# A planner's assumptions about transfer time and instruction time, in a hybrid DeltaNet and attention layer on one core

## The chip, the cores and the metric

The kernel runs on one core of a Trainium2 chip. The metric is device time in microseconds (us); below, the median of several executions. Five engines take part, each with a queue that it works through strictly in order: PE (TensorE, matmul), DVE (VectorE), ACT (ScalarE), POOL (GpSimd) and SP (SyncE), which here issues all the transfers.

## The reference

One layer over a sequence of 2048 rows of width 1024, in float32. After an RMS norm one projection feeds two groups of heads, whose outputs are concatenated, projected and added to the input:

```python
h = rms_norm(x, norm_w)
proj = h @ w_in
(dn_q, dn_k, dn_v, dn_z, dn_beta, dn_decay, sw_q, sw_k, sw_v, sw_z) = split(proj)
# A: 4 heads of 128, gated delta rule, forward and backward over the sequence
qkv = silu(depthwise_conv5(concat(dn_q, dn_k, dn_v)))
t_inv = inverse(eye + tril(k_beta @ k.T * decay, -1))      # per chunk
v_new = u_i - w_i @ state                                  # scan over chunks
state = state * exp(g_last) + k_dec.T @ v_new
dn = rms_norm(fwd + bwd, dn_out_norm_w) * silu(dn_z)
# B: 8 query heads of 64 over 2 kv heads, window |i-j| <= 128, rotary, sink logit
sw = windowed_gqa_with_sinks(sw_q, sw_k, sw_v, ...) * silu(sw_z)
out = x + concat(dn, sw) @ w_out
```

## The kernel before

The sequence is cut into 16 chunks of 128 rows. Products that need precision are split: an operand is rounded by ACT to a high part in the type fp32r, DVE takes the rest as a low part, and PE does three matmuls (high by high, low by high, high by low) in place of one.

**Phase A** (to about 680 us) loads and normalises x (`xprep_rows`, `xprep`), projects keys and values (`pq_kv`, L210 to L212), queries (`pq_q`) and the feature-major columns (`pf_c`, `pf_z`, L199 to L201), applies the convolution as four DVE instructions per 512 columns (`acc`, L269), and does the window attention chunk by chunk (`attend`). Projected keys and values go to DRAM and come back in `kv_chunk` (`kv<-kv_d`, L327, then an ACT copy into `v2`, L330).

**Phase B** is a chain over the four DeltaNet heads. For head h, `pre_front(h)` transposes keys and values and forms the matrices (`gh` on PE, L702, then `ma` on DVE, L711; four of them sit in tiles called `xhi_h` and `xlo_h`), and stores them to DRAM (`m_d`, L716). `solve(h)` loads 32 by 32 blocks (`X`, `L`, L739 and L740) and inverts them on DVE in 31 steps of two instructions (`tm`, L749; `X`, L753). The result goes through DRAM (`x_d<-X`, L754; `xc<-x_d`, L765) into `invert(h)`, where DVE transposes (`xt`, L766) and copies blocks (`iv`, L776) and PE joins them (`pi`, L781). `scan(h)` then walks 16 steps in both directions (`pk`, `py`, `po` on PE; `r`, L823, and the state `S`, L842, on DVE; each step's `kqc` is loaded by L819). Names carry the head, direction and step: `r0_0_11` is head 0, forward, step 11. Meanwhile 32 units of the output projection of the attention half stand ready to fill PE (`unit`: load `mxs`, ACT `mhs`, DVE `mls` L591, load `xrs`, 12 matmuls `pcs` L596 to L598, DVE add into `xrs` L599, store `part`). Gate projections of phase A (`late_gates`: `zs`, `zhi`, `zlo`, `pf_z`, `zo`) fill PE around the first solve. At the end `out_pair` multiplies the DeltaNet half.

The order in which each engine sees its instructions is not the order of this text. `set_order` collects all instructions with their dependencies, gives each a duration (`cost`), gives each edge between engines a lag (`LAG`, `SAME`), and list-schedules them, several times backward and forward (`plan`). The best of the later forward plans becomes a chain of order-only dependencies on every engine (`add_manual_dep`). For a transfer the lag from issue to landing is `LAG["SP"]` plus `move`, the time on the planner's bus, both in ns:

```python
move[k] = count / piece * (8 + 0.148 * piece) / 16
lag = LAG[eng[k]] + move[k] + late[k] if k < n else 0
```

`count` is the transfer's elements and `piece` the contiguous run, at most 2048. No order is recorded across engines: on the chip an instruction starts when its own queue reaches it and its operands are there. So the planner's numbers cost no device time themselves; they only decide what stands behind what.

## Time and profile before

| | |
|---|---|
| median of 3 runs | 1264.82 us (1262.38 to 1266.28) |
| profiled execution, span | 1268.0 us |
| PE busy | 1210.5 us (95%) |
| DVE busy | 953.7 us (75%) |
| ACT busy | 725.8 us (57%) |
| POOL busy | 529.2 us (42%) |
| transfers | 206.39 MB, 163 GB/s over the span |
| mean granted PE clock | 0.989 |

The profiled execution's own time is its span; the median of the runs is 3.2 us below it. A busy share is a mean over stages: in phase A PE and, in the convolution, DVE are busy nearly all the time, in phase B PE waits at single places. Matmuls overlap in the record, so a PE that reads as busy need not be at its peak; start-to-start distances tell its pace. An idle time of an engine stands in brackets in a timeline, with what ended it.

### The profile page before, as it was taken

To read this page: it belongs to the slowest core of one execution; us is meant where nothing else is said; L and a number is where in the kernel's file an instruction comes from. 1 tells how busy PE (TensorE), PEld (TensorE's weight loads), DVE (VectorE), ACT (ScalarE), POOL (GpSimd) and SP (SyncE) were. 2 spreads that over 40 slices of the span, in tenths; PEclk is the share of its full clock that TensorE was granted. 3 is DMA by queue.
4 is the path that set the end of the run, shared out by engine and by line. 5 is a ranking of instruction groups with operands and counts; after the bars stand their busy time and mean duration, and the time that the engine had idled before them with its cause. 6 is when DMAs were issued, how large, how long until landed. Compare 5 with 4: busy or idle time off the path is not lost.

```text
span 1268.0 us, 22351 instructions
## 1 busy us (share of the span) xinstructions
PE 1210.5 (95%) x7018; PEld 1037.4 (82%) x7018; DVE 953.7 (75%) x2320; ACT 725.8 (57%) x2167; POOL 529.2 (42%) x845
## 2 busy tenths in 40 slices
PE   6999999999999999999999998999889899999898
PEld 5998888788889988887777777888789689888776
DVE  4523689999854379999995587698769779876765
ACT  6432476666534367766665438658557845685421
POOL 2243454763302276556422304613742441670541
PEclk9999999999999999999999999999889999999999
DMA  7553243513544434431016848967955875854785
GB/s 259 172 160 125 75 154 100 173 60 102 166 145 125 144 110 137 137 96 55 34 51 207 238 141 245 264 189 207 268 166 174 236 200 152 242 175 122 238 269 199
DMA packets 232294, 206.39 MB, mean 163 GB/s; under 512 B 49137, under 2 KB 181873, under 8 KB 232177
## 3 DMA queue, kind: packets, MB, share of 16 engines
q1 hardware_dynamic: 232176, 204.97, 53.0%
q8 instruction: 56, 0.92, 0.3%
q14 instruction: 62, 0.50, 0.1%
HBM read 139.84 MB, written 65.08 MB: 162 GB/s over the span
## 4 chain that ended last, share of the span: by engine, by line
PE 67%; DVE 13%; DMA 9%; ACT 4%; issue 3%; POOL 1%; SPq 1%; DVEq 0%; ACTq 0%; POOLq 0%
PE pf_c L199 5%; PE pf_c L201 5%; PE pf_c L200 5%; PE pf_z L199 4%; PE pf_z L200 4%; PE pf_z L201 4%; PE pi L781 3%; PE pq_q L212 2%; PE pq_q L211 2%; PE pt L390 2%; PE pq_q L210 2%; DMA xc<-x_d 2%; PE py L830 2%; PE po L839 2%; PE pcs L596 2%
## 5 line engine op out<-in xcount | busy, mean ns | idle before, releaser
L199 PE MATMUL pf_c<-xhi,wh_c 128*128 128x512 f32 x384 | 155.7, 405 | 0.8 <-DVE acc L269 0.8
L200 PE MATMUL pf_c<-xlo,wh_c 128*128 128x512 f32 x384 | 154.7, 403 | 0.0
L201 PE MATMUL pf_c<-xhi,wl_c 128*128 128x512 f32 x384 | 154.3, 402 | 0.0
L269 DVE SCALAR_TENSOR_TENSOR acc<-pf_c,cw,acc 128x512 f32<-128x512 f32 (+1 forms) x192 | 140.8, 742 | 2.6 <-POOL acc L259 0.7
L385 POOL TENSOR_SCALAR pr<-pr,st 128x384 f32<-128x384 f32 (+1 forms) x128 | 79.4, 639 | 98.0 <-DVE st L383 71.2
L394 ACT ACTIVATE ph<-pt 128x512 fp32r<-128x512 f32 x92 | 53.0, 595 | 60.5 <-PE pt L390 51.5
L376 ACT ACTIVATE pr<-pr,st 128x384 f32<-128x384 f32 (+1 forms) x128 | 76.2, 597 | 17.8 <-DVE st L372 17.4
L199 PEld LDWEIGHTS pf_c<-xhi,wh_c 128*128 128x128 f32 x384 | 72.5, 189 | 13.5 <-DVE acc L269 1.3
L201 PEld LDWEIGHTS pf_c<-xhi,wl_c 128*128 128x128 f32 x384 | 72.3, 188 | 12.9
L200 PEld LDWEIGHTS pf_c<-xlo,wh_c 128*128 128x128 f32 x384 | 72.4, 188 | 11.6
L835 ACT ACTIVATE yk<-py,ck 128x128 f32<-128x128 f32 x120 | 43.9, 366 | 62.0 <-PE py L830 61.2
L372 DVE CUSTOM_DVE_ANT_0 pr<-s,mask,sink 128x384 f32<-128x384 f32 (+1 forms) x128 | 73.4, 593 | 2.5 <-PE s L371 1.0
L211 PE MATMUL pq_q<-wh_q,xlo 128*128 128x256 f32 x256 | 72.1, 282 | 0.0
L212 PE MATMUL pq_q<-wl_q,xhi 128*128 128x256 f32 x256 | 71.9, 281 | 0.0
L210 PE MATMUL pq_q<-wh_q,xhi 128*128 128x256 f32 x256 | 71.4, 280 | 0.0
L390 PE MATMUL pt<-ident,pr 128*128 128x128 f32 x368 | 69.5, 274 | 1.8 <-DVE pl L395 1.1
L395 DVE TENSOR_TENSOR pl<-pt,ph 128x512 fp32r<-128x512 f32 x92 | 61.6, 681 | 6.1 <-ACT ph L394 5.6
L390 PEld LDWEIGHTS pt<-ident,pr 128*128 128x128 f32 x368 | 47.8, 140 | 20.4 <-DVE pl L395 4.4
L596 PE MATMUL pcs<-wohs,mhs 128*128 128x512 f32 x128 | 58.3, 456 | 4.4 <-ACT mhs L590 2.7
L692 POOL TENSOR_TENSOR nk<-ssk,pw 128x4 f32<-128x4 f32 x16 | 16.5, 1029 | 106.8 <-DVE ssk L691 106.6
L597 PE MATMUL pcs<-wohs,mls 128*128 128x512 f32 x128 | 56.1, 438 | 1.7 <-DVE mls L591 1.7
L598 PE MATMUL pcs<-wols,mhs 128*128 128x512 f32 x128 | 55.0, 429 | 0.0
(324 smaller groups left out, 4029.4 us busy)
## 6 DMA issues: line engine op xcount, KB each, us to landing
kqc<-kq_d SPq DMA_DIRECT2D x120, 128.0 KB, 3.1
ws_c<-wt SPq DMA_DIRECT2D x48, 256.0 KB, 3.5
xr<-x SPq DMA_DIRECT2D x16, 512.0 KB, 5.3
k_q<-kq_d SPq DMA_DIRECT2D x16, 512.0 KB, 5.6
mxs<-mix_sw SPq DMA_DIRECT2D x32, 256.0 KB, 3.7
xrs<-x SPq DMA_DIRECT2D x32, 256.0 KB, 3.7
part<-xrs SPq DMA_DIRECT2D x32, 256.0 KB, 2.6
xrd<-part SPq DMA_DIRECT2D x32, 256.0 KB, 4.1
```

Of the source, the lines that this page charges most:

```text
L199: T.matmul(ps, hi[:, k, cs], xhi[b][:, k], start=(k == 0), stop=False)
L200: T.matmul(ps, hi[:, k, cs], xlo[b][:, k], start=False, stop=False)
L201: T.matmul(ps, lo[:, k, cs], xhi[b][:, k], start=False, stop=(k == KC - 1))
L210: T.matmul(ps[:, :n], xh, hi[:, k, :n], start=(k == 0), stop=False)
L211: T.matmul(ps[:, :n], xl, hi[:, k, :n], start=False, stop=False)
L212: T.matmul(ps[:, :n], xh, lo[:, k, :n], start=False, stop=(k == KC - 1))
L269: V.scalar_tensor_tensor(av, ps[:, lo:], cw[:, i, k : k + 1], av, ALU.mult, ALU.add)
L372: V.tensor_tensor_reduce(pr[j][:, :n], ps[:, :n], mask[:, lo * P : hi * P], 1.0, sink[:, hh : hh + 1], ALU.add, ALU.min, accum_out=nm[:, j ...
L376: A.activation(pr[j][:, :n], pr[j][:, :n], AF.Exp, bias=nm[:, j : j + 1], scale=-1.0, accum_out=den[:, j : j + 1])
L385: G.tensor_scalar(pr[j][:, :n], pr[j][:, :n], den[:, j : j + 1], 1.0, ALU.mult, ALU.mult)
L390: T.transpose(pt[:, j], pr[j][:, (kb - lo) * P : (kb - lo + 1) * P], ident)
L596: T.matmul(ps, mh[:, k], wh[:, k], start=(k == 0), stop=False)
```

## The change

The planner gets other numbers; no instruction is added, taken out or altered. The lag of a transfer goes from 2400 to 3000 ns and its bus time is multiplied by 1.1. The cost of an ACT instruction gets a base by its source (45 ns from PSUM, 85 from SBUF, where it was 60), and other additions for a scalar operand, for a second output and for a strided PSUM source. POOL gets a cheaper broadcast multiply (1.6 in place of 2.1 ns per element), a cheaper copy on up to 32 partitions, and a cost for small two-tensor instructions that grows up to 8 elements instead of 4. A matmul in fp32r goes from 0.441 to 0.445 ns per column.

```diff
-LAG = {"PE": 205, "DVE": 140, "Activation": 160, "Pool": 120, "SP": 2400}
+LAG = {"PE": 205, "DVE": 140, "Activation": 160, "Pool": 120, "SP": 3000}
...
-                return max(112, 0.441 * m + 4)
+                return max(112, 0.445 * m + 4)
...
-            short = len(o[0].ap) > 2 and o[0].ap[-1][1] <= 64
-            return 60 + 0.86 * m + 85 * (scalars > 0) + 110 * (len(o) > 1) + 100 * short
+            src = ins[0]
+            psum = src.tensor.name in tiles and "PSUM" in str(tiles[src.tensor.name].space)
+            apart = psum and len(src.ap) > 2 and src.ap[-2][0] > src.ap[-1][1]
+            return (45 if psum else 85) + 0.86 * m + 100 * (scalars > 0) + 85 * (len(o) > 1) + 110 * apart
...
-            return 350 + 165 * min(m, 4) if m <= 16 else 180 + 2.1 * m
-        return 190 + 1.02 * m
+            if m <= 16:
+                return 350 + 160 * min(m, 8)
+            return 180 + (1.6 if any(a.ap[-1][0] == 0 for a in ins) else 2.1) * m
+        return (70 if o[0].ap[0][1] <= 32 else 190) + 1.02 * m
...
-            move[k] = count / piece * (8 + 0.148 * piece) / 16
+            move[k] = 1.1 * count / piece * (8 + 0.148 * piece) / 16
```

The order changes on every engine. Three places matter below.

The first is ACT near the start of phase A. `xhi` is a rounded block of x that PE is about to multiply, `v2<-kv0` the first use of keys and values that have gone through DRAM. Before:

```order
L190 ACTIVATE wh_q0_0_431<-ws_q0_0_4_441 128x2x256
L330 ACTIVATE v2_158<-kv0_1075 128x2x64
L142 ACTIVATE xhi0_227<-xt0_3_0_388 128x4x128
L154 ACTIVATE xr1_1_565,rs1_561<-xr1_1_565 128x1024
L288 ACTIVATE sgkv2_377<-pq_kv2_352 128x272
L142 ACTIVATE xhi0_227<-xt0_3_1_395 128x4x128
```

With the change:

```order
L190 ACTIVATE wh_q0_0_431<-ws_q0_0_4_441 128x2x256
L142 ACTIVATE xhi0_227<-xt0_3_0_388 128x4x128
L288 ACTIVATE sgkv2_377<-pq_kv2_352 128x272
L142 ACTIVATE xhi0_227<-xt0_3_1_395 128x4x128
L154 ACTIVATE xr1_1_565,rs1_561<-xr1_1_565 128x1024
L330 ACTIVATE v2_158<-kv0_1075 128x2x64
```

The copy that needs the round trip through DRAM now stands behind both blocks of x.

The second is DVE at the end of the solve of head 1, whose last instruction is the `X1` row with `tm1_30`. Before:

```order
L749 TENSOR_TENSOR tm1_30_10372<-L1_10275,X1_10276 128x31
L694 TENSOR_TENSOR bp2_11356<-beta_4894,ssk2_11354 128x2x4
L842 SCALAR_TENSOR_TENSOR S0_0_14_9676<-S0_0_13_9636,egt_4922,po0_0_14_9668 128x128
L753 TENSOR_TENSOR X1_10276<-X1_10276,tm1_30_10372 128x31
L711 SCALAR_TENSOR_TENSOR ma2_0_11512<-gh2_0_0_11548,bp2_11356,v2_q_7736 128x2x128
L823 SCALAR_TENSOR_TENSOR r0_0_15_9705<-pk0_0_15_9703,negc_4920,vs0_3_8017 128x128
```

With the change:

```order
L823 SCALAR_TENSOR_TENSOR r0_0_11_9499<-pk0_0_11_9497,negc_4920,vs0_2_7890 128x128
L753 TENSOR_TENSOR X1_10276<-X1_10276,tm1_29_10369 128x2x30
L694 TENSOR_TENSOR bp2_11356<-beta_4894,ssk2_11354 128x2x4
L749 TENSOR_TENSOR tm1_30_10372<-L1_10275,X1_10276 128x31
L842 SCALAR_TENSOR_TENSOR S0_1_10_9490<-S0_1_9_9450,egt_4922,po0_1_10_9482 128x128
L753 TENSOR_TENSOR X1_10276<-X1_10276,tm1_30_10372 128x31
```

The solve ended at step 14 of head 0's scan and now ends at step 11 of it, and the first transpose of the inverse (`xt1_0_0`) stands 26 rows behind it before and 27 now.

The third is DVE early in the solve of head 2, at the addition of unit 11 of the output projection (`xrs11`), which needs a loaded block. Before:

```order
L749 TENSOR_TENSOR tm2_1_11875<-L2_11865,X2_11866 128x60
L753 TENSOR_TENSOR X2_11866<-X2_11866,tm2_1_11875 128x30x2
L749 TENSOR_TENSOR tm2_2_11878<-L2_11865,X2_11866 128x87
L753 TENSOR_TENSOR X2_11866<-X2_11866,tm2_2_11878 128x29x3
L599 TENSOR_TENSOR xrs11_0_11742<-xrs11_0_11742,pcs11_0_11744 128x512
L823 SCALAR_TENSOR_TENSOR r1_0_4_10794<-pk1_0_4_10792,negc_4920,xlo_h_9050 128x128
L749 TENSOR_TENSOR tm2_3_11881<-L2_11865,X2_11866 128x112
L753 TENSOR_TENSOR X2_11866<-X2_11866,tm2_3_11881 128x28x4
```

With the change:

```order
L749 TENSOR_TENSOR tm2_2_11878<-L2_11865,X2_11866 128x87
L753 TENSOR_TENSOR X2_11866<-X2_11866,tm2_2_11878 128x29x3
L749 TENSOR_TENSOR tm2_3_11881<-L2_11865,X2_11866 128x112
L753 TENSOR_TENSOR X2_11866<-X2_11866,tm2_3_11881 128x28x4
L842 SCALAR_TENSOR_TENSOR S1_0_5_10847<-S1_0_4_10805,egt_4922,po1_0_5_10839 128x128
L599 TENSOR_TENSOR xrs11_0_11742<-xrs11_0_11742,pcs11_0_11744 128x512
L842 SCALAR_TENSOR_TENSOR S1_1_5_10867<-S1_1_4_10826,egt_4922,po1_1_5_10859 128x128
L823 SCALAR_TENSOR_TENSOR r1_0_6_10876<-pk1_0_6_10874,negc_4920,xlo_h_9050 128x128
```

From the unit's `mls11` to this addition it is 12 rows before and 18 now, and the rows of the head-1 scan up to step 5 now stand ahead of it.

## The prediction

> **What bounds the kernel now.** I read the page's busy line first, then the windows by stage, then who waits for whom on PE, and last the chain of waits around the long waits.

> ```profile
> PE 1210.5 (95%) x7018; PEld 1037.4 (82%) x7018; DVE 953.7 (75%) x2320; ACT 725.8 (57%) x2167; POOL 529.2 (42%) x845
> PE 67%; DVE 13%; DMA 9%; ACT 4%; issue 3%; POOL 1%; SPq 1%; DVEq 0%; ACTq 0%; POOLq 0%
> ```

> The chain that ended last is PE for two thirds and transfers for 9%. No instruction changes, so PE's work stays; only its idle time (1268.0 - 1210.5 = 57.5 us) and what its clock loses can move. Where these lie, the windows say (columns: length, then busy time with count of PE, weight loads, DVE, ACT and POOL, granted PE clock, DMA share, GB/s):

> ```profile
> 0.00:40.00 40.00, 28.62 (x186) 26.80 (x187) 16.64 (x29) 22.70 (x49) 11.82 (x33) 0.96 0.82 280
> 480.00:680.00 200.00, 197.28 (x988) 159.43 (x988) 192.40 (x437) 137.45 (x347) 106.90 (x161) 1.00 0.29 96
> 680.00:760.00 80.00, 77.25 (x362) 62.28 (x361) 50.83 (x138) 37.85 (x146) 14.09 (x13) 1.00 0.65 185
> 760.00:800.00 40.00, 35.52 (x197) 29.43 (x196) 32.01 (x95) 29.58 (x118) 21.57 (x45) 0.96 0.85 247
> 880.00:920.00 40.00, 33.17 (x203) 29.05 (x202) 30.75 (x93) 26.16 (x106) 25.13 (x47) 0.91 0.94 262
> 920.00:960.00 40.00, 36.76 (x250) 34.16 (x250) 29.34 (x85) 22.17 (x73) 14.90 (x28) 0.91 0.57 169
> 1000.00:1040.00 40.00, 34.36 (x191) 29.17 (x192) 26.76 (x80) 20.20 (x68) 24.15 (x59) 0.91 0.76 203
> ```

> Phase A has almost nothing to give: from 480 to 680 us PE is busy for 197.3 of 200 us and DVE for 192.4. The open places are the start and the head chain of phase B, and there each long wait also costs clock: at 0.91 over 40 us the clock loses 0.09 x 40 = 3.6 us of full-speed time. Who is waited for:

> ```profile
> PE gh L702 <- DVE ma L711: 4.3, 4, 2.6
> PE gh L702 <- DVE xlo_h L711: 2.0, 1, 2.0
> PE pk L821 <- DVE S L842: 3.8, 4, 3.2
> PE pi L781 <- DVE iv L776: 3.6, 1, 3.6
> PE pq_kv L210 <- DVE xlo L143: 2.6, 1, 2.6
> ```

> DVE is named, but behind the last three stands a transfer that landed after its user's turn had come.

> **The change, part by part.** The planner's landing time (2400 ns plus bus time) becomes 3000 ns plus 1.1 times it. From the formula: `kv` has 128 pieces of 256 elements, so 0.37 us of bus and 2.77 us in all, now 3.40; `xc` 2.81, now 3.45; `x_d` 3.68, now 4.40; `xrs` 3.07, now 3.74. The trace's medians from issue to landing:

> ```profile
> kv<-kv_d SPq DMA_DIRECT2D x16, 128.0 KB, 2.9
> xc<-x_d SPq DMA_DIRECT2D x32, 64.0 KB, 4.0
> x_d<-X SPq DMA_DIRECT2D x4, 512.0 KB, 6.4
> xrs<-x SPq DMA_DIRECT2D x32, 256.0 KB, 3.7
> ```

> The old numbers were short of all four, the new ones fit `kv` and `xrs` and still miss `x_d` by 2 us. Each moves by only 0.6 to 0.7 us, less than the waits below, so what counts is how far the order really moved, and I take that from the order at three places.

> *Start.* The chain at 22.63 us, and ACT behind it:

> ```profile
> 22.63 4.04 DMA kv<-kv_d
> 25.17 0.63 ACT L190 ACTIVATE wh_q<-ws_q 128x512 fp32r<-128x512 f32 x1 [1.66 <-DMA ws_q<-wq]
> 26.69 0.31 ACT L330 ACTIVATE v<-kv 128x128 fp32r<-128x128 f32 x1 [0.89 <-DMA kv<-kv_d]
> 26.91 0.58 ACT L142 ACTIVATE xhi<-xt 128x512 fp32r<-128x512 f32 x1
> ```

> The copy `v<-kv` waits for its transfer; `xhi` queues behind it, DVE's `xlo` behind that, and PE waits 2.6 us. With the change both `xhi` blocks stand ahead of that copy, so the first can start at 25.8 us rather than 26.9, and SP issues the `ws_q` load two places earlier (two issues of some 0.4 us), which takes most of the other wait. Bounds: 0 and the 2.6 us of the wait. I take -2, since PE is saturated from there to 480 us and no other wait takes it over.

> *Head 1, solve to inverse.*

> ```profile
> 858.93 0.35 DVE L823 SCALAR_TENSOR_TENSOR r<-pk,negc,vs 128x128 f32<-128x128 f32 x1 [0.48 <-PE pk L821]
> 882.43 6.82 DMA x_d<-X
> 882.87 0.34 DVE L823 SCALAR_TENSOR_TENSOR r<-pk,negc,vs 128x128 f32<-128x128 f32 x1
> 889.27 4.05 DMA xc<-x_d
> 896.11 2.05 PE L781 MATMUL pi<-iv,g 128*128 128x128 f32 x8 [3.64 <-DVE iv L776]
> ```

> The two `r` rows are steps 11 and 15 of head 0's scan. The solve's last row stood beside step 15; now it stands beside step 11, 882.9 - 858.9 = 24 us earlier by this trace's clock. Store and load take 6.8 + 4.1 = 10.9 us, so they lie under steps 12 to 15, and PE's 3.6 us go, with the clock's 3.6 us. Bounds: 0 (the next chain, the end of head 0's scan into `gh` and `ma` of head 2, ends as late) and -7.2. PE waits 2.6 us at most for that next chain by the row above, so I give back about 2: -5.

> *Head 2, unit 11.*

> ```profile
> 924.46 6.88 DMA xrs<-x
> 926.93 0.25 DVE L753 TENSOR_TENSOR X<-X,tm 128x87 f32<-128x87 f32 x1
> 931.41 0.69 DVE L599 TENSOR_TENSOR xrs<-xrs,pcs 128x512 f32<-128x512 f32 x1 [4.23 <-DMA xrs<-x]
> 934.11 0.80 PE L821 MATMUL pk<-S,kqc 128*128 128x128 f32 x2 [3.24 <-DVE S L842]
> ```

> DVE stands 4.2 us before an addition whose block has not landed; queued behind are `r` and `S` of the scan and the solve itself, so PE's `pk` gets its state 3.2 us late, and the window's clock loses 3.6 us more. The change puts 6 more DVE rows between `mls11` and this addition, at 0.25 to 0.35 us each some 1.8 us, and the scan's `S1_1_3`, for which PE waited, now stands far ahead of it. Bounds: 0 (the load also slides in SP's queue) and -6.8. I take -3, nearer the middle, since 1.8 us cover less than half of 4.2.

> [...]

> *Head 0, the cost.* Here the change takes cover away. Between the last `gh` of head 0 and the first `pi`, PE has 237 matmuls of 512 columns before and 190 now, since late gates moved ahead of `pre_front(0)`. One takes 0.23 us, by two neighbours:

> ```profile
> 889.15 0.39 PE L598 MATMUL pcs<-wols,mhs 128*128 128x512 f32 x1
> 889.38 0.40 PE L596 MATMUL pcs<-wohs,mhs 128*128 128x512 f32 x1
> ...
> 716.51 0.48 DVE L711 SCALAR_TENSOR_TENSOR ma<-gh,bp,v_q 128x256 f32<-128x256 f32 x1
> 729.80 1.11 DVE L742 COPY L<-X 64x1024 f32<-64x1024 f32 x1
> 767.82 0.19 DVE L753 TENSOR_TENSOR X<-X,tm 128x31 f32<-128x31 f32 x1
> 779.40 0.31 DVE L766 STREAM_TRANSPOSE xt<-xc 128x128 f32<-128x128 f32 x1 [0.80 <-DMA xc<-x_d]
> 787.90 0.89 PE pi L781 x8
> ```

> So 47 x 0.23 = 10.8 us of cover go; four more `gh` now stand there, which leaves about 10 us. The chain there took 787.9 - 716.5 = 71.4 us. It is not at its floor: DVE is busy for 50.8 of 80 us in that stage, and from the first `xt` to `pi` 8.5 us pass, because copies of `iv` stand between `ma` rows of head 1, which the change puts earlier. Bounds: -1 and +10. I take +2, since those 8.5 us hold the two transposes, a dozen copies and 12 `ma` rows of 0.4 us (4.8 us), and the latter are what leaves.

> *Elsewhere.* Head 2's solve keeps its place (from its copy into `L` to its end 172 DVE rows before, 181 now), and from its end to `xt2_0_0` 36 rows shrink to 26; unit 10's `mls` and addition move closer, 13 rows to 7. Bounds: 0 and one more wait like unit 11's (3.2). I take +1. The new costs for ACT, POOL and PE show in no place of their own. Phase A from 40 to 680 us stays at zero: PE's work hides it; where DVE fell behind there, PE's idle time of 2.7 us in 200 would grow.

> Sum: -2 - 5 - 3 + 2 + 1 = -7 us on the profiled span, 1268.0 to 1261; carried to the median, which lies 3.2 us lower, 1264.8 - 7 = 1258.

> **The rivals.**

> (1) *The waits stay.* What a transfer takes depends on load, and a fixed lag does not follow it: `xrs` has a median of 3.7 us and took 6.9 us at the very place where DVE waited. Then the three waits reappear at other units and heads, only the start's -2 holds, and the time is 1263. For it speaks that `x_d` is still planned 2 us short; against it that the solve of head 1 moved by 24 us, far more than any landing varied. [...]

> (2) *Slower: head 0's inverse becomes the wait.* If the chain from the last `ma` of head 0 to the first `pi` stays at 71.4 us, PE's cover of some 56 us leaves it idle 10 us longer than now, with a window's clock loss of up to 3.6 us, and the later heads queue behind it. Start -2, this +10 and +1.8 for half that clock loss, and nothing of the other gains, since head 1's solve starts later too: about 1275. It decides from a chain of 61 us on. The busy share of DVE and the removed `ma` rows speak against it, the ten microseconds of lost cover for it.

> (3) *Faster still.* Both phase-B waits vanish whole: -2 - 7.2 - 6.8 and head 0 at 0 give 1249.

> **How the numbers follow.** A run of this kernel can be told from no change from about 0.3% on, 3.8 us. I give the forecast 0.45, (1) 0.22, (2) 0.18 and (3) 0.15. The forecast's own range is 1253 to 1263; to hold 8 in 10 it must reach most of (2) and (3): 1247 to 1273. Below 1261.0 lie (3), most of the forecast (0.40) and a little of (1) (0.05): faster 0.60. Within lie most of (1), 0.15, and the forecast's upper end, 0.05: 0.20. Slower is (2) with a rest of (1): 0.20.

> **What will show it.** Right if PE's waits for `xlo` near 25 us and for `iv` at head 1's first `pi` are under 1 us, DVE has no wait of 4 us for `xrs<-x` in head 2's solve, and the clock from 880 to 960 us is above 0.95. Wrong if PE waits several microseconds for `iv` before head 0's `pi`, if new waits over 3 us stand in another head, or if DVE turns into the bound from 480 to 680 us.

## The result: slower, and the profile after

The changed kernel takes 1278.2 us (median of 4 runs, 1275.8 to 1280.5) against 1263.6 us (median of 4 runs, 1261.8 to 1266.3) for the kernel before. The ratio is 1.0123, with a 95% interval of 1.0086 to 1.0160: slower, by more than this measurement's 0.3%. The forecast was 1258 us, with a range of 1247 to 1273 us. Both its sign and its range were wrong.

The windows of the profile after, by the same stages as before, with 800 to 840 us in addition (columns as there: length, busy time with count of PE, weight loads, DVE, ACT and POOL, granted PE clock, DMA share, GB/s):

```profile
0.00:40.00 40.00, 28.67 (x203) 27.31 (x204) 17.73 (x32) 23.03 (x50) 14.15 (x36) 1.00 0.83 276
480.00:680.00 200.00, 196.92 (x982) 160.35 (x981) 186.83 (x426) 134.39 (x337) 111.67 (x160) 1.00 0.26 85
680.00:760.00 80.00, 75.97 (x355) 61.37 (x355) 45.82 (x123) 39.89 (x149) 14.36 (x14) 0.98 0.71 204
760.00:800.00 40.00, 27.60 (x125) 20.98 (x124) 29.94 (x86) 24.71 (x104) 8.85 (x8) 0.84 0.79 228
800.00:840.00 40.00, 33.94 (x202) 29.40 (x203) 26.45 (x77) 21.86 (x67) 25.66 (x60) 0.90 0.73 204
880.00:920.00 40.00, 37.05 (x255) 32.83 (x254) 34.09 (x115) 37.38 (x163) 26.16 (x49) 1.00 0.91 251
920.00:960.00 40.00, 36.44 (x269) 33.76 (x269) 28.18 (x81) 23.79 (x79) 17.93 (x30) 1.00 0.68 197
```

Two things are to be seen. The windows from 880 to 960 us are what the forecast hoped for: the clock is 1.00 where it was 0.91. And head 0's stage has broken down: from 760 to 800 us PE is busy for 27.6 us in place of 35.5, at a clock of 0.84 in place of 0.96, and from 800 to 840 us the clock is 0.90 in place of 1.00. This is that last window before:

```profile
800.00:840.00 40.00, 37.87 (x256) 34.02 (x255) 29.05 (x82) 25.35 (x81) 15.66 (x28) 1.00 0.80 238
```

PE's waits of the whole execution after the change, longest sums first after the one at the very start:

```profile
PE gh L702 <- DVE xlo_h L711: 6.1, 1, 6.1
PE pf_z L199 <- ACT zhi L240: 5.0, 3, 3.4
PE pcd L994 <- ACT mh0d L988: 3.6, 1, 3.6
```

The waits for `iv` at head 1 and for `xlo` at the start, of 3.6 and 2.6 us before, are gone from the head of this list. The wait for head 1's `ma` rows (in `xlo_h`) has grown from 2.0 to 6.1 us and the waits for the late gates' weights (`zhi`) from 1.0 to 5.0 us; a wait of 3.6 us near 1186 us, at the change to `out_pair`, is new.

A second profiled execution of the kernel before (the first experiment below) had a span of 1261.0 us, near the median of the runs less some 2 us around the span; the one of the prediction, 1268.0 us, lay above all but the longest runs. The ledger is therefore made against the second. It counts every matmul of the trace at its usual start-to-start distance (0.23 us for 512 columns in fp32r, and so for each form). That sum, called PE work, is 1153.8 us in either kernel. The ledger takes what time (us) passed beyond it while PE worked through a given piece of its work:

| PE work done | what lies there | before, first | before, second | after | after less second |
|---|---|---|---|---|---|
| 0 to 22 us | start | 17.6 | 18.3 | 15.8 | -2.5 |
| 22 to 660 us | phase A | 15.8 | 14.9 | 13.0 | -1.9 |
| 660 to 760 us | head 0's stage | 12.2 | 12.3 | 28.8 | +16.5 |
| 760 to 880 us | heads 1 and 2 | 26.6 | 21.8 | 17.4 | -4.4 |
| 880 us to the end | heads 2 and 3, output | 42.1 | 39.9 | 45.2 | +5.3 |

The sum is +13.0 us, the spans differ by 1273.8 - 1261.0 = 12.8 us. More than the whole difference arose in one stage, head 0's.

How its chain moved shows on DVE and PE of the profile after (the last `ma` of head 0, the copy into `L`, the last step of solve 0, the first transpose, the first `pi`):

```profile
724.71 0.48 DVE L711 SCALAR_TENSOR_TENSOR ma<-gh,bp,dc 128x256 f32<-128x256 f32 x1
740.25 1.02 DVE L742 COPY L<-X 64x1024 f32<-64x1024 f32 x1
788.16 0.90 DVE L753 TENSOR_TENSOR X<-X,tm 128x31 f32<-128x31 f32 x1
802.73 0.31 DVE L766 STREAM_TRANSPOSE xt<-xc 128x128 f32<-128x128 f32 x1 [1.50 <-DMA xc<-x_d]
805.22 2.04 PE L781 MATMUL pi<-iv,g 128*128 128x128 f32 x8
```

and of the profile before (its first `pi` in this detail; the group view that the prediction quoted starts with a later one):

```profile
717.69 0.48 DVE L711 SCALAR_TENSOR_TENSOR ma<-gh,bp,dc 128x256 f32<-128x256 f32 x1
784.14 1.06 PE L781 MATMUL pi<-iv,g 128*128 128x128 f32 x8
```

From the end of the last `ma` to the first `pi` it was 66 us and is 80 us. Of these 14 us the solve has 10.6: it ran from 734.9 to 768.0 us (33.1 us) and now runs from 745.4 to 789.1 us (43.7 us). In its stretch of DVE's queue stood 29 rows that are not its own (foreign rows, below); now it is 47, and 14 of the 18 new ones are head 1's `ma` rows.

### The profile page after: what moved, and what is told of

It is laid out like the page before. It is cut to its first block, busy times and chain, and to the rows that moved or that the text cites. A ratio compares the mean times of both kernels' runs of the same rounds, so it can differ in the third digit from the quotient of the medians.

```text
span 1273.8 us, 22361 instructions
## 1 busy us (share of the span) xinstructions
PE 1206.5 (95%) x7018; PEld 1036.1 (81%) x7018; DVE 951.3 (75%) x2320; ACT 727.2 (57%) x2167; POOL 535.4 (42%) x845
## 4 chain that ended last, share of the span: by engine, by line
PE 70%; DVE 14%; DMA 6%; ACT 3%; POOL 3%; issue 2%; SPq 1%; POOLq 0%; DVEq 0%; ACTq 0%
PE pf_c L201 5%; PE pf_c L199 5%; PE pf_c L200 5%; PE pf_z L199 4%; PE pf_z L200 4%; PE pf_z L201 4%; PE pi L781 3%; PE pt L390 3%; DVE acc L269 2%; PE pq_q L211 2%; PE pq_q L212 2%; PE pq_q L210 2%; PE pcd L994 2%; PE pcd L995 2%; PE pcd L996 2%
## 5 line engine op out<-in xcount | busy, mean ns | idle before, releaser
L385 POOL TENSOR_SCALAR pr<-pr,st 128x384 f32<-128x384 f32 (+1 forms) x128 | 84.0, 674 | 83.7 <-DVE st L383 57.0
L376 ACT ACTIVATE pr<-pr,st 128x384 f32<-128x384 f32 (+1 forms) x128 | 76.2, 597 | 21.6 <-DVE st L372 21.0
L199 PEld LDWEIGHTS pf_c<-xhi,wh_c 128*128 128x128 f32 x384 | 72.3, 188 | 12.8
L210 PE MATMUL pq_q<-wh_q,xhi 128*128 128x256 f32 x256 | 71.6, 280 | 0.0
L390 PEld LDWEIGHTS pt<-ident,pr 128*128 128x128 f32 x368 | 48.6, 140 | 20.1 <-DVE pl L395 3.7
L596 PE MATMUL pcs<-wohs,mhs 128*128 128x512 f32 x128 | 56.5, 441 | 6.3 <-ACT mhs L590 2.6
L199 PE MATMUL pf_z<-xhi,zhi 128*128 128x512 f32 x128 | 52.8, 417 | 5.5 <-ACT zhi L240 5.0
## 6 DMA issues: line engine op xcount, KB each, us to landing
kqc<-kq_d SPq DMA_DIRECT2D x120, 128.0 KB, 2.8
ws_c<-wt SPq DMA_DIRECT2D x48, 256.0 KB, 3.4
xr<-x SPq DMA_DIRECT2D x16, 512.0 KB, 5.4
k_q<-kq_d SPq DMA_DIRECT2D x16, 512.0 KB, 5.5
mxs<-mix_sw SPq DMA_DIRECT2D x32, 256.0 KB, 3.3
xrs<-x SPq DMA_DIRECT2D x32, 256.0 KB, 3.5
part<-xrs SPq DMA_DIRECT2D x32, 256.0 KB, 2.6
xrd<-part SPq DMA_DIRECT2D x32, 256.0 KB, 4.4
```

Source lines behind the costliest of these rows:

```text
L199: T.matmul(ps, hi[:, k, cs], xhi[b][:, k], start=(k == 0), stop=False)
L210: T.matmul(ps[:, :n], xh, hi[:, k, :n], start=(k == 0), stop=False)
L376: A.activation(pr[j][:, :n], pr[j][:, :n], AF.Exp, bias=nm[:, j : j + 1], scale=-1.0, accum_out=den[:, j : j + 1])
L385: G.tensor_scalar(pr[j][:, :n], pr[j][:, :n], den[:, j : j + 1], 1.0, ALU.mult, ALU.mult)
L390: T.transpose(pt[:, j], pr[j][:, (kb - lo) * P : (kb - lo + 1) * P], ident)
```

## The experiments

Times are medians; each ratio is to runs of the kernel before on the same chip.

**The kernel before once more.**

> The kernel before, unchanged, for a second profile. The first profiled execution (1268.0 us of span, about 1270 us of device time) lies above all 22 timed runs so far (1258.7 to 1268.9), so its waits may be partly chance. If the 4.2 us wait for xrs and the 3.6 us wait for iv are chance, this profile lacks them and its span is 1258 to 1264 us; if they belong to the order, they are here again at the same rows.

It took 1263.1 us, with a span of 1261.0 us. DVE's wait for `xrs` at unit 11 is 1.7 us in place of 4.2, and PE's wait for `iv` at head 1 is there again (DVE's row from the timeline, then PE's row from the table of waits):

```profile
929.23 0.69 DVE L599 TENSOR_TENSOR xrs<-xrs,pcs 128x512 f32<-128x512 f32 x1 [1.67 <-DMA xrs<-x]
...
PE pi L781 <- DVE iv L776: 3.8, 1, 3.8
```

So of the two waits in phase B on which the forecast built, the one for `iv` belongs to the order with its size. The one at unit 11 comes with the order too, but its size varies from execution to execution: in three kernels below that keep the old order at that place (the mirror image, the start alone, and the start with head 1's solve packed) DVE stands 2.7, 2.4 and 2.0 us before the same row, and with the whole change it does not stand there. The first profile's 4.2 us was the longest of the five. The clock from 920 to 960 us was 1.00 here and 0.91 there.

**Pieces of the two orders.** Both plans are made, and a queue is joined from pieces of them, cut by the planner's time; a piece leaves out what an earlier one had. This changes no planner number on the way and cannot tie the queues into a knot, since every piece keeps its plan's order.

```diff
-    end, begin, queue = best
+    old, new = planned(False), planned(True)
...
+    for plan, until in pieces:
+        part = {e: [k for k in plan[2][e] if k not in done and plan[1][k] < until] for e in ENGINES}
+        for e in ENGINES:
+            queue[e] += part[e]
+            done.update(part[e])
```

The changed order with head 0's stage as before, and the mirror image:

> The changed plan everywhere, except that the stretch from the scores of attention chunk 10 (about 535 us of the planner's time) to head 0's first scan step is ordered by the plan of before. Theory A (the loss is made in head 0's stage alone, and the gains at the start and at heads 1 and 2 are independent of it): 1263.6 - 2 at the start - about 11 from 840 to 960 us + about 3 at the end = 1252 to 1257 us, and PE's waits of 6.1 us for xlo_h and 3.4 us for zhi are absent. Rival B (the gains at heads 1 and 2 exist only because PE arrives some 15 us late there, so that transfers have landed by then): the waits for iv at head 1 or for xrs at head 2 come back, and the time is 1261 to 1266 us.

> The mirror image: the plan of before everywhere, with only that stretch (attention chunk 10 to head 0's first scan step) in the changed order. Theory A: PE loses its 20 us from 720 to 840 us and the waits at heads 1 and 2 stay, so 1263.6 + 17 to 20 = 1280 to 1284 us. Rival B: PE's late arrival hides the later waits here too, 1263.6 + 20 - 11 = 1270 to 1275 us.

The first took 1273.3 us (1.0071, 1.0042 to 1.0099), the second 1278.7 us (1.0121, 1.0078 to 1.0163). The second bears theory A out, just under its 1280 to 1284 us: the stage alone, in an otherwise old order, costs what the whole change costs, and the later waits do not hide it. The first missed both expectations. Its solve was 32.6 us long, as before the change, and PE's loss from 720 to 800 us 8.8 us (10.0 before, 22.6 with the whole change), but right behind the seam it lost 12.7 us: the units of the output projection that the changed plan has earlier were all queued there, and PE waited 4.3 us for `wohs`. A later seam avoids this:

> No redraw, but pieces of the two orders joined: the changed order up to the scores of attention chunk 9, the order of before from there to step 11 of head 0's scan, the changed order to the end of head 1's scan, the order of before to the end. Theory A2 (each stage's loss or gain belongs to its own piece of the order, so the terms of the start and of heads 1 and 2 can be kept without head 0's loss): 1264.5 - 2.5 - 3 in phase A - 5 to 7 from 840 to 960 us = 1252 to 1257 us. Rival F (behind a seam the waits form anew, as from 800 to 840 us in the first joined order): 1262 to 1270 us.

It took 1266.7 us (1.0017, 0.9989 to 1.0045): no difference from before, as rival F had it. Head 0's stage cost 12.8 us, as before, and its first `pi` came at 785.5 us, so the loss goes with the stage's order. But the gains did not add up: 760 to 880 us of PE work gained 3.9 us on the second profile, phase A gave back 2.9 us behind its seam, and the end 6.6 us. These are the windows of 760 to 800 us with the stage alone new (the mirror image), and in this last kernel, whose stage is old:

```profile
760.00:800.00 40.00, 32.70 (x152) 25.24 (x150) 31.70 (x93) 25.45 (x113) 9.20 (x8) 0.90 0.67 191
```

```profile
760.00:800.00 40.00, 35.52 (x195) 29.69 (x194) 32.22 (x96) 29.45 (x118) 20.71 (x42) 0.96 0.84 244
```

**Which numbers do it.** The change in parts, and steps on either side of it:

```diff
-LAG = {..., "SP": 2400}
+LAG = {..., "SP": 3000}
...
-            move[k] = count / piece * (8 + 0.148 * piece) / 16
+            move[k] = 1.1 * count / piece * (8 + 0.148 * piece) / 16
```

> Before with the landing numbers alone (3000 ns and 1.1 times the bus time). Its order has the attention tail 10 to 15 us of PE work later and head 0's last gh at 689 us of PE work (679 before, 692 with the whole change). Theory A: this is the part that loses, 1273 to 1280 us. Rival C (any new numbers redraw the order and each stage's loss is chance, no part carries it): anything from 1255 to 1280 us, without the same PE waits from 720 to 840 us as with the whole change.

> Before with the new durations alone (ACT, POOL and PE costs). Its order leaves head 0's stage almost as before (last gh at 677 us of PE work). Theory A: no loss there, 1260 to 1267 us. Rival C: it moves by 5 us or more in either direction, at places that the whole change does not share.

> The whole change except the factor 1.1 on the bus time. In its order 20 foreign DVE rows stand inside solve 0 (29 before, 47 with the whole change) and 233 matmuls of 512 columns between head 0's last gh and first pi (237 before, 190 with the whole change). Theory D (the order of head 0's stage has two forms, and which of them the planner falls into decides, not the sizes of the new numbers): solve 0 takes 28 to 33 us, PE loses 14 us or less from 720 to 840 us, and the time is 1255 to 1267 us. Rival E (the new numbers are wrong for this chip wherever they act, as the landing part and the duration part each were slower alone): 1272 to 1280 us.

> Before with only the factor 1.1 on the bus time, some 0.03 to 0.2 us for the usual transfer. In its order 51 foreign DVE rows stand inside solve 0 and 202 wide matmuls in the cover. Theory D: this smallest part falls into the second form, solve 0 takes 42 to 45 us, PE loses 25 us or more from 720 to 840 us, and the time is 1272 to 1282 us. Rival E: a tenth of the bus time is a small part of the new numbers, so 1264 to 1268 us.

> The whole change with a landing lag of 3300 ns, further in the same direction. In its order 27 foreign DVE rows or so stand inside solve 0 and about 220 wide matmuls in the cover. Theory D: the first form again, solve 0 takes 31 to 35 us, 1255 to 1268 us. Rival E: more of the same, 1278 to 1286 us.

> Before with a landing lag of 2500 ns in place of 2400, nothing else. Theory C (any new number redraws the order; the order of before is a good draw, and what a draw costs has little to do with whether the number is nearer to the trace): 4 to 20 us slower than before, 1268 to 1285 us, at places of its own in phase B. Rival E (the new numbers are what costs, so a tenth of a microsecond costs a sixth of it at most): 1262 to 1267 us.

> Before with a landing lag of 2300 ns, a step in the other direction. Theory C: slower as well, 1268 to 1285 us. Rival E: the other direction, so no loss or a gain, 1258 to 1266 us.

| planner numbers | us | ratio, interval | solve 0, us | head 0's stage | rest, less second profile |
|---|---|---|---|---|---|
| landing lag and bus time alone | 1268.6 | 1.0031 (1.0008 to 1.0055) | 42.9 | 21.0 | -4.5 |
| durations alone | 1272.1 | 1.0064 (1.0041 to 1.0087) | 32.5 | 15.6 | +3.6 |
| all but the factor 1.1 | 1288.1 | 1.0179 (1.0146 to 1.0213) | 32.0 | 17.7 | +21.4 |
| the factor 1.1 alone | 1276.5 | 1.0088 (1.0056 to 1.0120) | 45.5 | 27.7 | -0.6 |
| all, with 3300 ns | 1282.8 | 1.0134 (1.0110 to 1.0158) | 31.9 | 15.0 | +17.1 |
| 2500 ns alone | 1265.2 | 1.0002 (0.9986 to 1.0018) | 31.0 | 11.5 | +2.6 |
| 2300 ns alone | 1280.4 | 1.0110 (1.0070 to 1.0149) | 32.4 | 17.2 | +16.2 |

(The last two columns are the excess over PE's counted work as in the ledger: 12.3 us is the second profile's value for the stage, and the rest is all other stages, less their 94.9 us there.)

What follows. In head 0's stage the orders fall into two forms, as theory D said: with 47 or more foreign rows in solve 0 it takes about 43 us or more, with 20 to 29 of them 31 to 33 us, and the factor 1.1 alone, the smallest part, tips it over. But the form does not decide the time: of the three kernels in the short form with the new durations two were the slowest of the seven, through phase A and heads 1 to 3 (theory D expected at most 1268 us of them). Theory A had put the loss into the landing numbers alone (1273 to 1280 us) and none into the durations alone; both missed, as the first two rows show. Rival E does not hold either: 100 ns less landing time, a step away from the change, costs 1.1%, about as much as the change itself, while 100 ns more costs nothing, where theory C had expected a loss. So what these runs bear out is the core of theory C: each new set of numbers redraws the order of the whole program, and what the draw costs at a stage has no visible relation to how near the number is to the trace. Of these seven sets and the whole change none was faster than before.

**What in head 0's stage makes the loss.** Five kernels start from the changed order and take one suspected cause from it each. The first is planned with one more rule, which puts `ma` rows behind the end of solve 0:

```diff
+    for k in rows[8:]:
+        nxt[solved].append((k, 0))
+        prv[k].append((solved, 0))
+    best = plan(kept, True)
```

> The whole change, and one more rule for head 1's ma rows on DVE (L711): from the ninth on they start after the last row of head 0's solve. 32 foreign DVE rows stand inside solve 0 in place of 47, the cover stays at 188 wide matmuls. Theory D1 (the rows moved into the solve stretch the chain): solve 0 takes 33 to 36 us in place of 43.7, the first pi comes 7 to 10 us earlier and the time is 1266 to 1272 us. Rival D2 (PE's lost cover sets the loss: gh, zlo and woss are late whatever DVE does in the solve): the solve is shorter but PE waits for ma instead, 1275 to 1284 us.

1282.4 us (1.0136, 1.0101 to 1.0172). The solve ended at 782.9 us, 6 us earlier, but DVE's queue then held the same `ma` rows ahead of the first transpose, which came at 804.9 us; the first `pi` came no earlier, at 806.9 us:

```profile
782.75 0.19 DVE L753 TENSOR_TENSOR X<-X,tm 128x31 f32<-128x31 f32 x1
...
804.94 0.30 DVE L766 STREAM_TRANSPOSE xt<-xc 128x128 f32<-128x128 f32 x1
...
806.95 0.64 PE L781 MATMUL pi<-iv,g 128*128 128x128 f32 x2
```

D1 falls: taking these rows out of the solve saves nothing. The time is in the range of D2, which puts the loss down to PE's lost cover (the work that PE still has to do ahead of the first `pi`); PE's waits for rows of `ma` in this stage are 9.8 us, 8.4 with the whole change.

The second moves two `wols` rows and one `mls` row of DVE behind the last `ma` rows; the third leaves most of solve 0's arithmetic out, with every row of every queue in its place:

```diff
-            n = 31 - c
+            n = 31 - c if h else 1
...
```

> The changed order with one piece of DVE's queue altered: the two rows of wols (which waited 3.6 us for the load of woss) and one of mls stand behind head 1's last seven ma rows instead of between them. Theory W (PE's named waits are the loss: its longest, 6.1 us in gh, comes from a DVE that stands at wols): that wait falls under 2.5 us, the half clock behind it shrinks, and the time is 1269 to 1274 us. Theory K (the chain from head 0's last ma over solve, store and load to the first pi has become longer than PE's other work there, and a wait that is taken away returns as another before that pi): the first pi stays within 2 us of 805 us and the time is 1275 to 1280 us.

> The changed order row for row, but each step of head 0's solve updates only the next row of X instead of all rows below, so most of that solve's arithmetic is left out: its 62 DVE rows take some 0.19 us each in place of 22.6 us in all, about 10 us less. Theory K: the first pi comes 8 to 11 us earlier, PE's loss from 720 to 840 us falls by about as much, and the time is 1267 to 1271 us. Theory W: the weights zs and woss land as late as before, so PE stands in the same places, 1274 to 1279 us.

1277.9 us (1.0104, 1.0071 to 1.0138) and 1276.9 us (1.0102, 1.0066 to 1.0139). In the first of these two the wait for `xlo_h` shrank from 6.1 to 1.8 us and one for `mhs` came in its place (PE's waits from 720 to 830 us):

```profile
PE pcs L596 <- ACT mhs L590: 6.3, 2, 4.3
PE pf_z L199 <- ACT zhi L240: 5.0, 2, 3.8
PE gh L702 <- DVE ma L711: 2.4, 2, 2.1
...
PE gh L702 <- DVE xlo_h L711: 1.8, 1, 1.8
```

The short solve is the most telling. One of the two groups of the solve's rows (`tm`, 31 rows; DVE's busy time in the stretch of the solve) with the changed order, and with the arithmetic left out:

```profile
745.38:789.06 43.68, 11.35 (x31) 0.95 0.55 162
```

```profile
747.06:790.80 43.74, 5.64 (x31) 0.96 0.53 156
```

With the other group the solve's own work fell from 22.6 to 11.9 us, and the solve took 43.7 us, as with the whole change. What had been work became waiting at the foreign rows (DVE's longest waits in that stretch with the changed order, then with the arithmetic left out; all of them sum up to 8.1 and 18.3 us):

```profile
DVE zlo L241 <- ACT zhi L240: 2.8, 4, 1.9
DVE zo L246 <- ACT zo L245: 2.0, 1, 2.0
DVE ssk L691 <- ACT jk L690: 1.4, 1, 1.4
```

```profile
DVE zlo L241 <- ACT zhi L240: 8.2, 7, 1.9
DVE ssk L691 <- ACT jk L690: 5.4, 2, 5.0
DVE zo L246 <- ACT zo L245: 3.3, 3, 2.6
```

So solve 0 is not paced by its own work. Its rows stand in DVE's queue behind rows that need ACT's and PE's progress, and it ends when those have got there. Theory K had the first `pi` 8 to 11 us earlier by this; it came at 808.7 us, so K's picture of a chain with a length of its own falls, and W falls with the run before it.

The fourth pulls the solve's last seven steps ahead of the rows that need the latest products of PE, and with them the store, the first loads and, on PE, the first `pi`; the same remedy at head 1 of the order of before is told further down.

> The changed order with some 30 rows moved: on DVE the last seven steps of head 0's solve stand ahead of the rows fed by gh1_2_1, zo4_3 and gh1_0 (they stood between and behind these), wols and mls behind head 1's last ma rows, on PE the first pi ahead of the first unit of the output projection, on SP the store of X0 and the first two loads of xc as much earlier. Theory T (a tie of the queues: the solve ends only when PE has made the products that DVE's rows ahead of its last step need; in the changed order that is gh1_0_1, with 4.0 us of PE work left to the first pi, before it is gh1_1_1, with 17.3 us, against some 16 us for store, load and first pi): now it is gh1_2_0 with 12.9 us left, the solve ends at 780 to 783 us in place of 789, the first pi starts at 796 to 800 in place of 805, and the time is 1267 to 1272 us. Rival W2 (PE's other work there is out of weights until woss lands near 795 us, so PE waits just as long): 1275 to 1280 us.

1281.3 us (1.0135, 1.0100 to 1.0170). The solve ended at 783.6 us, but its store stood in SP's queue behind a store of a gate (`zdn<-zo`) that itself had moved back, and left at 787.7 us; the loads of `woss` slid behind it, DVE waited for them ahead of the first transpose, and the first `pi` came at 809.0 us, after 10.2 us of waiting. The time lies above both expectations:

```profile
787.05 0.59 SPq L247 DMA_DIRECT2D zdn<-zo  x1
787.73 0.38 SPq L754 DMA_DIRECT2D x_d<-X  x1
...
805.29 0.30 DVE L766 STREAM_TRANSPOSE xt<-xc 128x128 f32<-128x128 f32 x1
...
809.03 2.05 PE L781 MATMUL pi<-iv,g 128*128 128x128 f32 x8 [10.24 <-DVE iv L776]
```

The fifth gives the gate weights four buffers in place of two, the order kept:

```diff
-                    st = wz.tile([P, 2, P], F32, tag="zst", name=f"zs{i}_{b}_{kk}", bufs=2)
+                    st = wz.tile([P, 2, P], F32, tag="zst", name=f"zs{i}_{b}_{kk}", bufs=4)
```

> The changed order row for row, with four buffers instead of two for the gate weights zs, so that a load no longer waits until DVE has made zlo of the one before the last. Theory Z (the solve's rows stand behind zlo rows, and these are paced by the loads of zs: ACT waited 18.5 us for zs from 720 to 830 us, DVE 11.9 us for zhi, PE 5.0 us): these waits halve at least, PE's two waits for zhi (3.4 and 1.4 us) go, the solve ends 6 to 10 us earlier, and the time is 1266 to 1272 us. Rival (the loads leave no earlier, since SP's queue holds them behind stores that wait, or gh and woss take the waits over): 1275 to 1280 us.

1279.4 us (1.0130, 1.0102 to 1.0159). ACT's waits for `zs` from 720 to 830 us fell from 18.5 to 15.2 us only (with the whole change, then with four buffers):

```profile
ACT zhi L240 <- DMA zs<-wt: 18.5, 10, 2.7
...
ACT zhi L240 <- DMA zs<-wt: 15.2, 9, 3.0
```

SP's queue held the loads in their old places among stores that wait: a store `zdn<-zo` left at 758.1 us, 9.6 us after the end of the row ahead of it, and the next two loads of `zs` behind it at 758.5 us. In all five kernels head 0's stage cost 29.8 to 34.2 us, as with the change (28.8) or more. So none of the rows that they moved makes the loss alone.

What all five share is the lost cover. Between head 0's last `gh` and the first `pi` their PE queues hold 182 to 190 matmuls of 512 columns, 190 with the whole change and 237 before. In the plans and joins of this study the stage cost 11.5 to 17.7 us with 220 to 246 of them (but for the join that lost its time right behind its seam) and 21.0 us or more with 182 to 202. The number of foreign rows does not go along in the same way: with 32 of them, in the kernel with the added rule and in the one with the pulled tail, the stage was dearest, 34.2 and 32.3 us. That the lost cover is the cause is not shown, since no run gave it back alone; nor is it shown how the loss splits between it and the longer chain.

**A version that beats both.** The start's term came back in every kernel with the changed start, and the two plans hold exactly the same instructions up to 43.5 us of the planner's time in the one and 44 us in the other. So the order of before, with that first piece from the changed plan:

> The order of before, with only its first 44 us of the planner's time (rows to about the first block of x) in the changed order, joined where the two plans hold exactly the same instructions. If the term of the start is right by itself: 2 to 2.6 us less, 1261.5 to 1262.5 us, against 1264.3 for before, and PE's wait near 25 us is 1.2 us in place of 2.6 to 3.3. If it is taken back in phase A: 1264 to 1265 us.

1261.1 us (12 runs) against 1264.6: ratio 0.9968, 0.9945 to 0.9990. The first 22 us of PE work cost 16.0 in place of 18.3 us. This is the fastest kernel of the study. On top of it, head 1's solve with its last rows packed closer:

> Before with the changed start (as in the kernel that measured 0.9968) and the same remedy at head 1: the last 13 rows of its solve stand one by one between the next 13 foreign DVE rows, the first transposes and copies of iv ahead of one addition, the store of X1 and the first two loads of xc some 6 us earlier on SP. Theory T: PE's wait of 3.9 us for iv near 892 us falls under 1 us and most of the half clock behind it goes, the scan's rows lose about 1 us to the packed solve: 1261.1 - 3 to - 5 = 1256 to 1258 us. Rival: the next chain (scan's end into head 2's ma) takes the wait over, 1260 to 1263 us.

1264.8 us (1.0013, 0.9986 to 1.0040), above both expectations. The long wait for `iv` is gone (no wait of PE from 850 to 930 us is over 1.6 us), but 800 to 880 us of PE work cost 21.6 us against 20.1 without it: shorter waits at `pi`, `gh` and `pcs` took its place.

## Why the prediction was wrong

*Start, -2:* right. Measured -2.5 us in the whole change, -2.3 us alone, and nothing took it back.

*Head 1, -5, and head 2, unit 11, -3:* right as a mechanism, with one size off. PE's wait for `iv` vanished and the clock from 880 to 960 us is 1.00, as the prediction named for a sign. The two together gain 4.4 us on the second profile (9.2 on the first, against the 8 forecast). The difference lies at unit 11: its wait of 4.2 us was taken from one execution, and 1.7 to 2.7 us were seen in four others with the same order there.

*Head 0, the cost, +2:* the step that failed, and it turned the sign. Measured +16.5 us in that stage. The lost cover was counted rightly (47 matmuls, some 10 us), and then nearly all of it was set against "12 `ma` rows of 0.4 us (4.8 us), and the latter are what leaves". This offset was worth nothing. Its stretch was misread: the first `pi` of before stands at 784.1 us, not at 787.9, so the chain was 66 us and not 71.4, and from the first transpose to the first `pi` it was 4.7 us and not 8.5, with 4 `ma` rows in it and not 12 (8 up to 787.9 us). These 4 did leave, and the 4.7 us became 2.5; yet the chain grew from 66 to 80 us. Rows that leave one place in a queue arrive in another, and the prediction did not look where: 14 more `ma` rows stood now inside the solve. Taking them out of it again gained nothing either. The prediction also treated DVE's idle share as room (50.8 busy of 80 us). The shortened solve shows that this idle time is no room: it is waiting at foreign rows in a queue that keeps its order. So the cost went beyond the +10 that was its bound, in every kernel that kept the changed stage; which part of it is the lost cover and which the longer chain stays open.

Rival (2) had the place, the direction and a time near the result (1275, measured 1278.2), and was given 0.18. Its mechanism was only half right: the cover did go, but the chain did not keep its length, it grew by 14 us. That its time came near is in part luck: it took 11.8 us for the stage, where 16.5 were measured, and no gain at heads 1 and 2, where 4.4 us were gained.

*Elsewhere, +1:* mis-sized. From 880 us of PE work to the end the change lost 5.3 us. By the same count it lost 7.3 us from 880 to 920 us of PE work, where PE's waits are up to 2.1 us each, and gained 2.7 in the next 40; another 2.3 us lie from 1060 to 1080, where `out_pair` begins, at the wait of 3.6 us for `mh0d`. No step named these places. Phase A, taken at zero, gained 1.9 us.

Of the four signs named for right, three came out (no DVE wait of 4 us for `xrs` in head 2's solve, the clock above 0.95, no wait for `iv` at head 1) and one nearly (1.2 us for `xlo`, where under 1 was asked). One sign for wrong came out with them: new waits over 3 us at other places. The three signs that came out all lay where the gains were, not in head 0's stage.

Rival (1), that the waits stay, is refuted at head 1. Its ground, that a fixed lag does not follow the load, is there at head 0: the loads of `zs` took up to 6.9 us and those of `woss` up to 7.1 us from issue to landing, where the planner, by its formula with the new numbers, allows 3.5 and 3.7 us; the seven loads of `zs` issued from 743 to 763 us, at a DMA share of 0.22, took 2.4 to 2.5 us, and the three from 763.7 us on, at a share of 0.93, 5.2 to 6.9 us. But before the change they took up to 6.7 and 6.4 us, so this alone does not make the difference.

## What to carry to other kernels

A planner's number is no edit at one place: each new set redraws the order of the whole program, and neighbouring sets here scatter from 1.000 to 1.018 of the time before, so a forecast from three places that look better is a forecast from three draws out of many. Where a new order improves one stage, cut that piece out and join it to the order that is good elsewhere, at a point where both plans hold the same instructions; here that gave 0.3% at the start from a change that cost 1.2%, while the joins at two later places lost behind their seams what they were to gain. When rows leave a stretch of a queue, find where in it they arrive, and look at a wait in a second profile, before either is counted as a gain.

## What the runs showed of the hardware

```profile
794.02 1.57 PE L702 MATMUL gh<-k_q 128*128 128x256 f32 x4 [2.02 <-DVE xlo_h L711]
...
790.00:794.58 4.58, 2.56 (x21) 2.29 (x20) 4.46 (x18) 3.79 (x13) 3.38 (x11) 1.00 1.10 323
794.58:797.99 3.41, 3.41 (x16) 3.23 (x15) 3.28 (x6) 1.88 (x4) 3.12 (x7) 0.50 0.98 258
797.99:802.00 4.01, 4.01 (x31) 3.75 (x31) 3.42 (x9) 2.65 (x9) 3.67 (x8) 1.00 0.94 248
```

In the 3.41 us ahead of that step PE had stood for 2.0 us. In the changed kernel the steps at half clock add up to 23.9 us from 742 to 825 us (one of 10.24 and four of 3.41 us), so its losses in head 0's stage are waits and clock together.
